# Diagonal and short block lengths of the second mixer as 32-token products, masked into a compact tile

## Chip, cores and metric

The kernel runs on one core of one Trainium2 chip. The metric is device time of one execution in microseconds. A core has a matrix engine (TensorE, PE in the profile; its weight loads stand apart as PEld), a vector engine (DVE), a scalar engine (ACT), a general engine (POOL) and a queue that issues transfers (SP). They run side by side and wait for each other through semaphores.

## What is computed

One step of a two-layer recurrent decoder for 512 prompt tokens and 32 sample tokens (8 sequences of 4). The change lies in the mixer of the second layer, HGRN2, which has 8 heads with 128 key and 128 value channels. For one head and a chunk of tokens, the reference computes attention with a decay that lies between the two tokens:

```python
    def step(S, inp):
        qc, kc, lc, ic = inp
        bc = jnp.cumsum(lc, axis=2)
        diff = bc[:, :, :, None, :] - bc[:, :, None, :, :]
        dec = jnp.exp(jnp.where(mask, diff, -jnp.inf))
        att = jnp.einsum('bhtsk,bhtk,bhsk->bhts', dec, qc, kc)
        o = (jnp.einsum('bhts,bhsv->bhtv', att, ic)
             + jnp.einsum('bhtk,bhkv->bhtv', qc * jnp.exp(bc), S))
```

Around it stand a projection (`xn @ w_in_c`, 32 column blocks of 128), a gate, an output projection and a feed-forward network; the first layer has two other mixers.

## The kernel before

**Layout.** Channels lie on the 128 partitions, tokens along the free dimension (512 prompt, then 32 sample tokens). A projection block is a chain of 128 x 128 weights against 272 tokens at a time, three products for each block of weights (high part of the weights with high and low part of the input, then low part of the weights): tiles `acc`, `wh`, `wl`. ACT makes `wh` from the loaded weights `wf` (line 202), DVE makes `wl` (line 205), SP issues the loads.

**One head (`mix`, from line 1447).** The decayed attention matrix A (tokens s on partitions, tokens t along the free dimension, four blocks of 128 tokens) is built by block length. First the diagonal: products of K and q0, of which the identity keeps the diagonal (tile `d0`, which the profile prints as `d`; trailing numbers are left out). Then for l = 0 to 6 and block length b = 1, 2, 4, ..., 64: products of K with every second block of Q of length b (tile `lv`), of which the mask `lmask[:, l]` keeps those where t lies in the block right after that of s. Between two levels K and Q are multiplied in place by decay products G (K on POOL, line 1477; Q on DVE, line 1478), so a level's products wait for the updates of the level ahead, and those updates wait until that level's products have read K and Q. The masked entries go into A by `copy_predicated` on DVE (line 1480); at b = 64 a plain copy on ACT does it (line 1485). The 32 sample tokens have their own small products (`d0s`; `ps[0:32, 4, 0:16]` at b = 1 and 2).

The products are made on 64 tokens of K by 64 columns: for each of the four blocks of 128 tokens, one product for each half (`g`) writes partitions 0 to 63 or 64 to 127 of the result. Each float32 product is two MATMUL and two LDWEIGHTS in the trace, so 8 products are x16 there.

**What sets the order.** During the heads every product of TensorE is chained in the order in which it is written (`in_order = "all"`). Between the levels a hand-written count of projection products of the next head is placed: `FILL = (27, 13, 13, 24, 10, 23, 5, 9, 4, 19)`, taken by `fill(FILL[l])`. They keep TensorE at work while POOL and DVE update K and Q. On the other engines a scheduler decides the order. `Am` holds two A tiles, used by turns; one quarter of each is cleared once, on POOL (line 1342). Results of the products lie in four PSUM buffers (tag `m`), used in turn. After the levels come transposes of V and K (`tr`, `trs`), the state products `ds` and the outputs `ops<-A,VT`, `ops<-Q,S`, `opsq` and `opsm`; the states of the sample group (`tail`, with `dss`) are done while the next head runs.

Of the kernel before, what the change touches and what calls it, by code (L numbers as in the profile page):

```python
# [11 lines left out]
F32 = mybir.dt.float32  # L12
F32R = mybir.dt.float32r
I32 = mybir.dt.int32
AF = mybir.ActivationFunctionType
OP = mybir.AluOpType
# [65 lines left out]
def consts_np():  # L82
    c = {}
    c["ident"] = np.eye(128, dtype=np.float32)
    b = np.zeros((128, 128), np.float32)
    b[:64, :64] = 1
    b[64:, 64:] = 1
    c["block64"] = b
    c["half32"] = np.repeat(b[:, ::64], 16, axis=1)
    z = np.zeros((128, 4, 128), np.float32)  # L90
    for q in range(4):
        z[32 * q, q, :64] = 1
        z[32 * q + 16, q, 64:] = 1
    c["spread"] = z
    r = np.ones((128, NT), np.float32)
    r[:, 0:SEQ:CH] = 0
    r[:, SEQ::NS] = 0
    c["reset"] = r
    i = np.arange(32)[:, None]
    t = np.arange(32)[None, :]  # L100
    strict, incl = (i < t).astype(np.float32), (i <= t).astype(np.float32)
    same = (i // 4 == t // 4).astype(np.float32)

    def rows(s, n):
        top = np.concatenate([s, n], 1)
        bot = np.concatenate([0 * s, n], 1)
        return np.concatenate([top, bot, top, bot], 0)

    def pair(flip):
        m = np.stack([rows(strict, incl), rows(strict * same, incl * same)], 1)  # L110
        return m.reshape(2, 2, 32, 2, 64)[:, ::-1].reshape(128, 2, 64) if flip else m

    c["smask"] = np.stack([pair(True), pair(False)], 1)
    c["upper"] = np.tile((np.arange(CH) < CH // 2)[:, None], (4, 1)).astype(np.float32)
    sel = np.zeros((32, 8), np.float32)
    sel[np.arange(32), np.arange(32) // 4] = 1
    c["seqsel"] = np.tile(sel, (4, 1))
    c["sum4"] = np.tile(np.eye(32, dtype=np.float32), (4, 1))
    s = np.arange(128)[:, None]
    lv = []  # L120
    for l in range(7):
        b = 1 << l
        t = np.array([x for x in range(128) if (x // b) % 2])[None, :]
        lv.append(((s // b) + 1 == t // b).astype(np.int32))
    c["lmask"] = np.stack(lv, 1)
    return {k: np.ascontiguousarray(v) for k, v in c.items()}


class Build:
# [13 lines left out]
    def fill(self, n):  # L143
        while n and self.work:
            try:
                next(self.work[0])
                n -= 1
            except StopIteration:
                self.work.pop(0)
# [1177 lines left out]
    def mixer1(self, xg):  # L1327
        nc, I = self.nc, self.i
        v = self.v
        TT, STT, TS = nc.vector.tensor_tensor, nc.vector.scalar_tensor_tensor, nc.vector.tensor_scalar  # L1330
        ACT = nc.scalar.activation
        PTT = nc.gpsimd.tensor_tensor
        p = self.open("m1")
        lmask = p.tile([128, 7, 64], I32, name="lmask")
        nc.sync.dma_start(lmask, I["lmask"])
        seqsel = p.tile([128, 8], F32, name="seqsel")
        nc.sync.dma_start(seqsel, I["seqsel"])
        sum4 = p.tile([128, 32], F32, name="sum4")
        nc.sync.dma_start(sum4, I["sum4"])
        Am = [p.tile([128, 4, 128], F32, name=f"A{i}") for i in range(2)]  # L1340
        for i in range(2):
            nc.gpsimd.memset(Am[i][64:128, :, 0:64], 0.0)
        qms = [p.tile([128, NB, 32], F32, name=f"qm{i}") for i in range(2)]
        for i in range(2):
            nc.gpsimd.memset(qms[i], 0.0)
# [18 lines left out]
        def tmp(name, shape=None, bufs=2):  # L1364
            return p.tile(shape or [128, NT], F32, tag=name, name=name, bufs=bufs)

        def blk(z, b, n):
            return z[:, 0:n].rearrange("p (m g b) -> p m g b", g=2, b=b)
# [60 lines left out]
        def tail(h, S0, KVs, G):  # L1429
            Vx = p.tile([96, NB, 128], F32R, tag="Vx", name="Vx")  # L1430
            PTT(Vx, KVs[:, 1, None, :].bitcast(F32).to_broadcast([96, NB, 128]),
                seqsel[0:96, :, None].to_broadcast([96, NB, 128]), OP.mult)
            PTT(S0, S0, G[4][:, SEQ // 4:, None].to_broadcast([128, NB, 128]), OP.mult)
            for q in range(2):
                yield
                bs = slice(4 * q, 4 * q + 4)
                ps = self.ms.tile([128, 4, 128], F32, tag="m", name="dss")
                self.mm(ps, KVs[:, 0], Vx[:, bs])
                TT(S0[:, bs], ps, S0[:, bs], OP.add)
            nc.sync.dma_start(self.o["hS_s"][h], S0)  # L1440
            self.norm_add(oh[h])
            done.append(h)
            if h < len(gates):
                combine(h)

        def mix(h, late):
            K, q0, Q, G, V = heads[h]
            S0 = tmp("S0", [128, NB, 128])
            nc.sync.dma_start(S0, I["hS"][h])
            A = Am[h % 2]  # L1450
            As = tmp("As", [32, 32])
            ps = self.ms.tile([128, 4, 64], F32, tag="m", name="d0")
            for c in range(4):
                for g in range(2):
                    ks = slice(128 * c + 64 * g, 128 * c + 64 * g + 64)
                    self.mm(ps[64 * g:64 * g + 64, c], K[:, ks], q0[:, ks])
            for g in range(2):
                r = slice(64 * g, 64 * g + 64)
                TT(A[r, :, r], ps[r], self.ident[r, None, r].to_broadcast([64, 4, 64]), OP.mult)
            ps = self.ms.tile([32, 32], F32, tag="m", name="d0s")  # L1460
            self.mm(ps, K[:, SEQ:], q0[:, SEQ:])
            TT(As, ps, self.ident[0:32, 0:32], OP.mult)
            for l in range(7):
                b = 1 << l
                ps = self.ms.tile([128, 5, 64], F32, tag="m", name="lv")
                for c in range(4):
                    for g in range(2 if b < 64 else 1):
                        ks = slice(128 * c + 64 * g, 128 * c + 64 * g + 64)
                        self.mm(ps[64 * g:64 * g + 64, c], K[:, ks],
                                blk(Q[:, 128 * c:128 * c + 128], b, 128)[:, :, 1])  # L1470
                if b <= 2:
                    self.mm(ps[0:32, 4, 0:16], K[:, SEQ:], blk(Q[:, SEQ:], b, 32)[:, :, 1])
                n = NT if b <= 2 else SEQ
                m = n // (2 * b)
                g2 = G[b][:, 0:2 * m].rearrange("p (m g) -> p m g", g=2)
                kv, qv = blk(K, b, n), blk(Q, b, n)
                PTT(kv[:, :, 0], kv[:, :, 0], g2[:, :, 1, None].to_broadcast([128, m, b]), OP.mult)  # L1477
                TT(qv[:, :, 1], qv[:, :, 1], g2[:, :, 0, None].to_broadcast([128, m, b]), OP.mult)
                if b < 64:
                    nc.vector.copy_predicated(  # L1480
                        A.rearrange("p c (m g b) -> p c m g b", g=2, b=b)[:, :, :, 1],
                        lmask[:, l, None, :].to_broadcast([128, 4, 64]).rearrange("p c (m b) -> p c m b", b=b),
                        ps[:, 0:4].rearrange("p c (m b) -> p c m b", b=b))
                else:
                    ACT(A[0:64, :, 64:], ps[0:64, 0:4], AF.Copy)
                if b <= 2:
                    nc.vector.copy_predicated(
                        blk(As, b, 32)[:, :, 1], lmask[0:32, l, 0:16].rearrange("p (m b) -> p m b", b=b),
                        ps[0:32, 4, 0:16].rearrange("p (m b) -> p m b", b=b))
                fill(FILL[l])  # L1490
                if late is not None and l in LATE:
                    next(late, None)
# [6 lines left out]
            for z in (V, K):  # L1499
                zt = tmp("KT" if z is K else "VT", [128, 4, 128], 1)  # L1500
                ps = self.ms.tile([128, 4, 128], F32, tag="m", name="tr")
# [7 lines left out]
            ps = self.ms.tile([32, 2, 128], F32, tag="m", name="trs")  # L1509
# [31 lines left out]
            for b in range(NB):  # L1541
                q = 32 * (b % 4)
# [8 lines left out]
            t = tail(h, S0, KVs, G)  # L1551
# [9 lines left out]
        for h in range(8):  # L1561
            if h < 7:
                work.append(project(h + 1))
            for g in GATES[h]:
                work.append(gate(g))
            late = mix(h, late)
            if h < 7:
                drain()
# [26 lines left out]
def prep(x_prompt, x_sample, state_rglru_conv, state_rglru_h, state_rwkv_shift, state_rwkv_S,  # L1595
# [9 lines left out]
    def tiles(w):  # L1605
        w = A(w)
        k, m = w.shape
        return C(w.reshape(k // 128, 128, m // 128, 128).transpose(2, 1, 0, 3)).reshape(m // 128, 128, k)

    d = consts_np()  # L1610
    x = np.concatenate([A(x_prompt).reshape(SEQ, D), A(x_sample).reshape(NB * NS, D)], 0)
    d["xT"] = C(x.T.reshape(KT, 128, NT).transpose(1, 0, 2))
# [75 lines left out]
```

## Time and profile before

| | |
|---|---|
| median of 3 runs | 1539.9 us (1539.0 to 1541.34) |
| profiled execution | 1541.22 us, span 1539.4 us |
| granted TensorE clock, mean | 0.971 |
| ACT busy | 552.5 us (36%) |
| POOL busy | 418.3 us (27%) |
| HBM read, written | 120.65 MB, 11.02 MB |

The span is the time from the first to the last instruction; the profiled execution's own time lies 1.8 us above it. Shares of busy time are means over stages with different limits: the mixer that is changed runs from about 800 to 1080 us of the span. A row "x16" of the timeline is 16 instructions one after the other, from the start of the first to the end of the last. "128*32 128x16" in a row of TensorE is a weight tile of 128 partitions by 32 columns and a moving tile of 16 columns.

### The profile page before, as it was taken

What the parts mean: (1) busy time and instruction counts of PE and PEld (TensorE: products, weight loads), DVE (VectorE), ACT (ScalarE), POOL (GpSimd) and SP (SyncE); (2) the same over time, 40 slices, a digit from 0 to 9 for tenths busy, and PEclk for the clock granted to TensorE, in tenths of its full rate; (3) what the DMA queues carried; (4) which work ended last, traced back from release to release, by engine and by line L of the source; (5) the groups of instructions that cost most, each with busy time, mean ns of one, the idle gap of its engine ahead of it and who ended that gap; (6) DMA issues with size and microseconds to landing.
All of it is one profiled execution on the core that took longest, in us unless ns stands there. A gap on an engine that the chain in (4) does not pass through costs nothing.

```text
span 1539.4 us, 33537 instructions
## 1 busy us (share of the span) xinstructions
PE 1465.2 (95%) x13872; PEld 1408.7 (92%) x13872; DVE 860.2 (56%) x1618; ACT 552.5 (36%) x997; POOL 418.3 (27%) x540
## 2 busy tenths in 40 slices
PE   6967888779999999999999999999999999999998
PEld 6857777669999999999999999999999999999997
DVE  7777555785544344334576667666674433444444
ACT  5634234354433233223352333333453322332224
POOL 3664535542110011001133434444431100110010
PEclk9978989889999999999999999999999999999999
DMA  4224311122232322322231232322242222223221
GB/s 158 70 71 104 105 38 36 49 80 93 83 96 83 90 89 84 96 83 91 85 120 58 85 98 85 106 87 90 97 124 90 89 86 87 90 90 90 84 75 59
DMA packets 92010, 133.86 MB, mean 87 GB/s; under 512 B 28976, under 2 KB 34864, under 8 KB 91728
## 3 DMA queue, kind: packets, MB, share of 16 engines
q1 hardware_dynamic: 91856, 131.71, 27.2%
q8 instruction: 109, 1.79, 0.5%
q14 instruction: 45, 0.37, 0.1%
HBM read 120.65 MB, written 11.02 MB: 86 GB/s over the span
## 4 chain that ended last, share of the span: by engine, by line
PE 84%; DVE 7%; ACT 3%; issue 2%; DMA 2%; POOL 1%; SPq 1%; DVEq 0%; POOLq 0%; ACTq 0%
PE acc L171 74%; PE lv L171 2%; PE ops L171 1%; PE ch L171 1%; DVE Z L842 1%; DVE t L571 0%; PE ds L171 0%; PE tr L1503 0%; DVE W L528 0%; PE nps L171 0%; DVE wl L205 0%; DMA S<-rS 0%; DMA x<-xT 0%; DMA wd<-down 0%; DVE Pd L653 0%
## 5 line engine op out<-in xcount | busy, mean ns | idle before, releaser
L171 PE MATMUL acc<-xg,wh 128*128 128x272 f32 x4544 | 888.1, 293 | 11.7 <-ACT xg L262 7.2
L171 PEld LDWEIGHTS acc<-xg,wh 128*128 128x128 f32 x4544 | 721.7, 191 | 21.7 <-ACT xg L262 7.5
L171 PE MATMUL acc<-xg,wl 128*128 128x272 f32 x2272 | 653.1, 293 | 0.2 <-DVE wl L205 0.2
L202 ACT ACTIVATE wh<-wf 128x512 fp32r<-128x512 f32 (+1 forms) x404 | 250.8, 621 | 655.8 <-PE acc L171 544.3
L171 PEld LDWEIGHTS acc<-xg,wl 128*128 128x128 f32 x2272 | 429.1, 190 | 4.9 <-issue 1.3
L205 DVE TENSOR_TENSOR wl<-wf,wh 128x512 fp32r<-128x512 f32 (+1 forms) x373 | 267.1, 716 | 192.2 <-ACT wh L202 166.2
L1207 POOL TENSOR_TENSOR S<-S,rstd 128x272 f32<-128x272 f32 x88 | 74.3, 845 | 645.3 <-ACT S L1206 645.2
L171 PE MATMUL acc<-h,wh 128*128 128x272 f32 x1280 | 236.9, 288 | 0.0
L171 PEld LDWEIGHTS acc<-h,wh 128*128 128x128 f32 x1280 | 198.0, 188 | 0.0
L171 PE MATMUL acc<-h,wl 128*128 128x272 f32 x640 | 176.7, 287 | 0.0
L171 PEld LDWEIGHTS acc<-h,wl 128*128 128x128 f32 x640 | 118.1, 188 | 0.0
L1210 DVE TENSOR_TENSOR hh<-acc,S 128x272 f32<-128x272 f32 x88 | 38.9, 442 | 127.2 <-PE acc L171 125.3
L171 PE MATMUL acc<-cat,wh 128*128 128x272 f32 (+2 forms) x512 | 100.2, 295 | 2.7 <-ACT wh L202 2.7
L171 PEld LDWEIGHTS acc<-cat,wh 128*128 128x128 f32 x512 | 82.7, 194 | 3.5 <-ACT wh L202 3.1
L1206 ACT ACTIVATE S<-t 128x272 f32<-128x272 f32 x88 | 37.8, 431 | 123.4 <-DVE t L1205 123.4
L1227 DVE TENSOR_TENSOR x<-acc,x 128x272 f32<-128x272 f32 x80 | 35.0, 439 | 83.3 <-PE acc L171 83.0
L1205 DVE TENSOR_TENSOR t<-acc,rstd 128x272 f32<-128x272 f32 x88 | 38.7, 441 | 70.7 <-PE acc L171 70.6
L171 PE MATMUL acc<-cat,wl 128*128 128x272 f32 (+2 forms) x256 | 74.2, 296 | 2.0 <-POOL wl L205 1.0
L280 POOL TENSOR_TENSOR ssq<-ssq,sq 128x544 f32<-128x544 f32 x33 | 46.5, 1410 | 93.4 <-ACT sq L279 93.0
L1477 POOL TENSOR_TENSOR K<-K,G 128x256 f32<-128x256 f32 (+1 forms) x48 | 39.8, 828 | 78.3 <-PE lv L171 78.3
L205 POOL TENSOR_TENSOR wl<-wf,wh 128x512 fp32r<-128x512 f32 x31 | 41.3, 1334 | 40.7 <-ACT wh L202 40.4
L171 PEld LDWEIGHTS acc<-cat,wl 128*128 128x128 f32 x256 | 49.2, 194 | 2.8 <-POOL wl L205 1.4
(341 smaller groups left out, 1506.9 us busy)
## 6 DMA issues: line engine op xcount, KB each, us to landing
wf<-gate SPq DMA_DIRECT2D x88, 256.0 KB
wf<-up SPq DMA_DIRECT2D x88, 256.0 KB
wf<-down SPq DMA_DIRECT2D x72, 256.0 KB
wf<-w_in_c SPq DMA_DIRECT2D x64, 256.0 KB
wf<-w_in_ab SPq DMA_DIRECT2D x44, 256.0 KB
x<-xT SPq DMA_DIRECT2D x16, 272.0 KB
wf<-w_out_ab SPq DMA_DIRECT2D x16, 256.0 KB
S<-hS SPq DMA_DIRECT2D x8, 512.0 KB
```

The source lines that it names most:

```text
L171: return self.seq(self.nc.tensor.matmul(out, lhsT, rhs, start=start, stop=stop, skip_group_check=True), chain)
L202: nc.scalar.activation(wh[:, :n], wf[:, :n], AF.Copy)
L205: eng.tensor_tensor(wl[:, :n], wf[:, :n], wh[:, :n].bitcast(F32), OP.subtract)
L280: eng.tensor_tensor(self.ssq, self.ssq, t, OP.add)
L842: nc.vector.tensor_copy(zc[par][q, e::2], cu[q])
L1205: nc.vector.tensor_tensor(t[:, c], ps, rs()[:, c], OP.mult)
L1206: nc.scalar.activation(S[:, c], t[:, c], AF.Silu)
L1207: nc.gpsimd.tensor_tensor(S[:, c], S[:, c], rs()[:, c], OP.mult)
L1210: nc.vector.tensor_tensor(hh[:, c], ps, S[:, c], OP.mult)
L1227: nc.vector.tensor_tensor(x[:, c], ps, x[:, c], OP.add)
L1477: PTT(kv[:, :, 0], kv[:, :, 0], g2[:, :, 1, None].to_broadcast([128, m, b]), OP.mult)
```

## The change

The products of the diagonal and of b = 1 to 16 are made on 32 tokens of K instead of 64. Each of the four groups of 32 tokens in a block of 128 writes its own 32 partitions of the result, that is, a quarter of the columns of the TensorE array: 32 columns for the diagonal, 16 for a level. At b = 32 there are two products of 32 by 32 for each block of 128, on the first and the third quarter. b = 64 stays.

The results of the diagonal and of b = 1 to 16 are masked into a compact tile `Ad` (128 x 4 x 32) instead of A. After b = 16, four copies on POOL lay the four quarters of `Ad` on the diagonal of A. At b = 32 two copies on ACT write A, in place of a masked copy on DVE. Both A tiles are cleared whole at the start. The mask shrinks to 5 levels of 16.

```diff
-    c["lmask"] = np.stack(lv, 1)
+    c["lmask"] = np.ascontiguousarray(np.tile(np.stack(lv, 1)[0:32, 0:5, 0:16], (4, 1, 1)))
...
-        lmask = p.tile([128, 7, 64], I32, name="lmask")
+        lmask = p.tile([128, 5, 16], I32, name="lmask")
...
-            nc.gpsimd.memset(Am[i][64:128, :, 0:64], 0.0)
+            nc.gpsimd.memset(Am[i], 0.0)
...
-            ps = self.ms.tile([128, 4, 64], F32, tag="m", name="d0")
+            quads = [slice(32 * q, 32 * q + 32) for q in range(4)]
+            ps = self.ms.tile([128, 4, 32], F32, tag="m", name="d0")
             for c in range(4):
-                for g in range(2):
-                    ks = slice(128 * c + 64 * g, 128 * c + 64 * g + 64)
-                    self.mm(ps[64 * g:64 * g + 64, c], K[:, ks], q0[:, ks])
-            for g in range(2):
-                r = slice(64 * g, 64 * g + 64)
-                TT(A[r, :, r], ps[r], self.ident[r, None, r].to_broadcast([64, 4, 64]), OP.mult)
+                for r in quads:
+                    ks = slice(128 * c + r.start, 128 * c + r.stop)
+                    self.mm(ps[r, c], K[:, ks], q0[:, ks])
+            Ad = tmp("Ad", [128, 4, 32])
+            TT(Ad, ps, sum4[:, None, :].to_broadcast([128, 4, 32]), OP.mult)
...
-                    for g in range(2 if b < 64 else 1):
-                        ks = slice(128 * c + 64 * g, 128 * c + 64 * g + 64)
-                        self.mm(ps[64 * g:64 * g + 64, c], K[:, ks],
-                                blk(Q[:, 128 * c:128 * c + 128], b, 128)[:, :, 1])
+                    Kc, Qc = K[:, 128 * c:128 * c + 128], Q[:, 128 * c:128 * c + 128]
+                    if b < 32:
+                        for r in quads:
+                            self.mm(ps[r, c, 0:16], Kc[:, r], blk(Qc[:, r], b, 32)[:, :, 1])
+                    elif b == 32:
+                        for r, t in ((quads[0], quads[1]), (quads[2], quads[3])):
+                            self.mm(ps[r, c, 0:32], Kc[:, r], Qc[:, t])
+                    else:
+                        self.mm(ps[0:64, c], Kc[:, 0:64], Qc[:, 64:128])
...
-                if b < 64:
+                if b < 32:
                     nc.vector.copy_predicated(
-                        A.rearrange("p c (m g b) -> p c m g b", g=2, b=b)[:, :, :, 1],
-                        lmask[:, l, None, :].to_broadcast([128, 4, 64]).rearrange("p c (m b) -> p c m b", b=b),
-                        ps[:, 0:4].rearrange("p c (m b) -> p c m b", b=b))
+                        Ad.rearrange("p c (m g b) -> p c m g b", g=2, b=b)[:, :, :, 1],
+                        lmask[:, l, None, :].to_broadcast([128, 4, 16]).rearrange("p c (m b) -> p c m b", b=b),
+                        ps[:, 0:4, 0:16].rearrange("p c (m b) -> p c m b", b=b))
+                elif b == 32:
+                    for r, t in ((quads[0], quads[1]), (quads[2], quads[3])):
+                        ACT(A[r, :, t], ps[r, 0:4, 0:32], AF.Copy)
                 else:
                     ACT(A[0:64, :, 64:], ps[0:64, 0:4], AF.Copy)
+                if b == 16:
+                    for r in quads:
+                        nc.gpsimd.tensor_copy(A[r, :, r], Ad[r])
```

What this does to the order of instructions is shown at three places of a head. On TensorE, where a head starts (`opsm` ends the head ahead, `d` is the diagonal, `lv` the level b = 1, and the `acc` rows are the next head's projection); lines with - are of before, with + of the change:

```order
 L171 MATMUL opsm<-sum_9503,Oi 128x32
-L171 MATMUL d_10146<-q_9990,K 64x64 x8
-L171 MATMUL d0s<-q_9990,K 32x32
-L171 MATMUL lv<-Q,K 64x64 x8
-L171 MATMUL lv<-Q,K 32x16
+L171 MATMUL d_10199<-q_10043,K 32x32 x16
+L171 MATMUL d0s<-q_10043,K 32x32
+L171 MATMUL lv<-Q,K 32x16 x17
 L171 MATMUL acc<-xg,wh 128x272 x2
 L171 MATMUL acc<-xg,wl 128x272
```

Twice as many products, of half the rows, stand at the same place, and the small product of the sample tokens now has the same shape as the others; nothing else moves on this engine.

On POOL, from the update of K at b = 8 to that at b = 64 in the first head (`G` are decay products of the next head), first before:

```order
L1403 TENSOR_TENSOR G<-G 128x32
L1403 TENSOR_TENSOR G<-G 128x16
L1477 TENSOR_TENSOR K<-K,G 128x16x16
L1403 TENSOR_TENSOR G<-G 128x8
L1403 TENSOR_TENSOR G<-G 128x4
L1477 TENSOR_TENSOR K<-K,G 128x8x32
L1477 TENSOR_TENSOR K<-K,G 128x4x64
```

and now:

```order
L1403 TENSOR_TENSOR G<-G 128x32
L1482 TENSOR_TENSOR K<-K,G 128x16x16
L1403 TENSOR_TENSOR G<-G 128x16
L1496 COPY A_9505<-Ad 32x4x32 x4
L1403 TENSOR_TENSOR G<-G 128x8
L1482 TENSOR_TENSOR K<-K,G 128x8x32
L1403 TENSOR_TENSOR G<-G 128x4
L1482 TENSOR_TENSOR K<-K,G 128x4x64
```

The four copies into A stand between the updates of K at b = 16 and b = 32; two of the G products have moved behind updates of K.

On ACT, in the same stretch of a head (`F`, `K` and `q` belong to the next head, `wh` are the projection's weights, `VT` comes after the levels), first before:

```order
L1384 ACTIVATE K<-fr 128x544
L202 ACTIVATE wh<-wf 128x512 x2
L1390 ACTIVATE q_9990<-fr 128x544
L1485 ACTIVATE A_9505<-lv 64x4x64
L1504 ACTIVATE VT<-tr 128x512
```

and now:

```order
L1384 ACTIVATE K<-fr 128x544
L202 ACTIVATE wh<-wf 128x512
L1491 ACTIVATE A_9505<-lv 32x4x32 x2
L202 ACTIVATE wh<-wf 128x512
L1390 ACTIVATE q_10043<-fr 128x544
L1493 ACTIVATE A_9505<-lv 64x4x64
L1515 ACTIVATE VT<-tr 128x512
```

The two copies of b = 32 stand between the two weight conversions.

## The prediction

> **What bounds the kernel now.** I read the page first: the busy times and the chain of work that ended last.
>
> ```profile
> PE 1465.2 (95%) x13872; PEld 1408.7 (92%) x13872; DVE 860.2 (56%) x1618; ACT 552.5 (36%) x997; POOL 418.3 (27%) x540
> PE 84%; DVE 7%; ACT 3%; issue 2%; DMA 2%; POOL 1%; SPq 1%; DVEq 0%; POOLq 0%; ACTq 0%
> ```
>
> TensorE carries 84% of the chain. This is a mean over the program, so I look at the changed mixer alone: two of eight windows of 35 us between 800 and 1080 us, then who waited for whom in that stretch.
>
> ```profile
> 835.00:870.00 35.00, 35.00 (x395) 32.06 (x395) 23.23 (x49) 12.03 (x25) 15.72 (x19) 1.00 0.28 89
> 870.00:905.00 35.00, 35.00 (x342) 32.94 (x341) 21.12 (x43) 11.33 (x23) 13.57 (x19) 1.00 0.26 83
> ...
> ACT wh L202 <- PE acc L171: 112.7, 49, 6.5
> POOL K L1477 <- PE lv L171: 89.3, 52, 4.2
> DVE wl L205 <- ACT wh L202: 25.0, 28, 1.6
> ```
>
> The columns of a window are PE, PEld, DVE, ACT and POOL busy, clock, DMA share and GB/s. TensorE is never idle, at full clock; DVE has 12 us of 35 free, POOL about 20. The two largest waits are others waiting for TensorE: ACT for a buffer of weights, POOL for the level's products. No wait of TensorE for another engine is among them. So here time is what TensorE's own instructions take, and the chain of one head shows them; its pieces run from one start to the next:
>
> ```profile
> 867.74 0.61 PE d L171 x16
> 868.35 0.18 PE d0s L171 x2
> 868.53 0.78 PE lv L171 x18
> ...
> 842.85 0.79 PE lv L171 x18
> 843.63 1.82 PE acc L171 x13
> 845.46 0.62 PE lv L171 x16
> 847.90 0.62 PE lv L171 x16
> 851.71 0.61 PE lv L171 x16
> 852.32 1.46 PE acc L171 x10
> 853.78 0.62 PE lv L171 x16
> 854.39 3.06 PE acc L171 x23
> 857.46 0.61 PE lv L171 x8
> ```
>
> (The first three belong to the head that follows.) What the change rewrites of a head, diagonal to b = 32, is 0.61 + 0.18 + 0.78 + 0.79 + 0.62 + 0.62 + 0.61 + 0.62 = 4.83 us of TensorE, eight times over 38.6 us. b = 64 (the last row, 0.61) stays.
>
> **How such a batch is priced.** A "pair" is a weight load with its MATMUL. Batches on parts of the array, from timeline rows (start, time, form, count) and the row that follows each:
>
> ```profile
> 865.23 0.64 PE L171 MATMUL opsq<-S,qm 128*32 128x128 f32 x16
> 865.80 0.39 PE L171 MATMUL acc<-xg,wh 128*128 128x272 f32 x1
> ...
> 279.40 0.43 PE L171 MATMUL ops<-Z,W 128*32 128x64 f32 x16
> 279.77 0.52 PE L171 MATMUL acc<-xg,wh 128*128 128x272 f32 x2
> ...
> 217.08 0.73 PE L171 MATMUL jps<-Yt,NTt 32*32 32x16 f32 x64
> 217.74 0.52 PE L171 MATMUL acc<-xg,wh 128*128 128x272 f32 x2
> ...
> 80.44 1.26 PE L171 MATMUL ndps<-KB,W 64*32 64x32 f32 x124
> 81.54 0.25 PE L171 MATMUL ndss<-W,KB 64*32 64x32 f32 x4
> ...
> 229.39 1.05 PE L171 MATMUL jps<-join,Zt 32*32 32x16 f32 x64
> 230.37 0.59 PE L171 MATMUL acc<-xg,wh 128*128 128x272 f32 x1
> ```
>
> First, rounds count, not pairs, as long as pairs lie on different parts: at b = 64 eight pairs on one half take 0.61, at b = 32 sixteen pairs on two halves 0.62. Second, 128x32 weights on the four quarters (the new form) run four abreast: 16 pairs, four rounds, took 0.57 with 128 columns (`opsq`) and 0.37 with 64 (`ops`). The 0.20 between them is 4 rounds of 64 columns, so 64 columns cost 0.05 a round and 0.37 - 4 x 0.05 = 0.17 is fixed: going over, first weights, draining. Third, a floor by pairs: `ndps` made 124 in 1.10 us, 8.9 ns each.
>
> **The change, part by part.** *A level at b = 4, 8, 16*: 32 pairs of 16 columns in 8 rounds. By columns alone 8 x 0.0125 + 0.17 = 0.27. By the floor 32 x 0.0089 = 0.28, plus some 0.11 for going over (estimated from `jps`: 0.66 - 64 x 0.0086) = 0.39. No row shows this form with so few columns. The dear end is the slower `jps`: (0.98 - 0.11) / 64 = 13.6 ns a pair, 0.55 for 32. I take 0.38, nearest to the fast `jps` and `ndps` rows, which have pairs as small as these. *b = 2*, 34 pairs: 0.40. *Diagonal, sample diagonal and b = 1*: 32 + 2 + 34 pairs, now of one weight shape, so the array goes over once. The old rows show what that costs: `d0s`, two pairs, took 0.18. I reckon 2 x 0.38 - 0.11 + 4 x 0.009 = 0.69, for 1.57 before. *b = 32*: 16 pairs on two quarters, 8 rounds of 32 columns: 8 x 0.025 + 0.17 = 0.37.
>
> New sum of a head: 0.69 + 0.40 + 3 x 0.38 + 0.37 = 2.60; saved 4.83 - 2.60 = 2.23 us, over eight heads **17.8 us**. With the cheap end (0.27 a level, 0.29 at b = 2, 0.55 for the first batch) a head is 2.02 and 22.5 us are saved; with 13.6 ns a pair it is 1.03 + 0.57 + 3 x 0.55 + 0.37 = 3.62, and 9.7 us are saved.
>
> *Does the saving reach the end?* The `acc` pieces between levels stay, and the updates of K and Q start when a level ends; cover and cover's need move together. What is new beside TensorE:
>
> ```profile
> 852.41 0.87 POOL L1477 TENSOR_TENSOR K<-K,G 128x256 f32<-128x256 f32 x1 [0.35 <-PE lv L171]
> 853.25 0.47 POOL L1403 TENSOR_TENSOR G<-G 128x8 f32<-128x8 f32 x2
> 854.49 0.67 POOL L1477 TENSOR_TENSOR K<-K,G 128x256 f32<-128x256 f32 x1 [0.76 <-PE lv L171]
> 858.21 0.97 POOL L1477 TENSOR_TENSOR K<-K,G 128x256 f32<-128x256 f32 x1 [3.06 <-PE lv L171]
> ...
> L1495 POOL COPY qm<-Q 128x32 f32<-128x32 f32 x8 | 1.7, 208 | 0.7 <-DVE Q L1478 0.7
> L1477 POOL TENSOR_TENSOR K<-K,G 128x256 f32<-128x256 f32 x40 | 31.6, 790 | 56.5 <-PE lv L171 56.5
> ...
> 853.32 0.63 ACT L202 ACTIVATE wh<-wf 128x512 fp32r<-128x512 f32 x1 [4.27 <-PE acc L171]
> 855.96 0.63 ACT L202 ACTIVATE wh<-wf 128x512 fp32r<-128x512 f32 x1 [2.01 <-PE acc L171]
> 858.10 0.38 ACT L1485 ACTIVATE A<-lv 64x256 f32<-64x256 f32 x1 [0.96 <-PE lv L171]
> ...
> 787.07 0.56 POOL L1342 MEMSET A<- 64x256 f32 x2
> 790.53 1.36 POOL L280 TENSOR_TENSOR ssq<-ssq,sq 128x544 f32<-128x544 f32 x1 [2.27 <-ACT sq L279]
> ```
>
> *Four POOL copies* of 128 elements a partition, each from 0.21 us (a copy of 32 elements) to 0.79 (a product of 256 elements, two sources); I take 0.3, by the copy, since they are copies of half the elements of the other: 1.2 us a head. They also wait for the masked copy of b = 16 on DVE. Behind them in the queue is K's update for b = 32, which TensorE awaits at b = 64 (857.46). From 853.5 (K's update ended at 853.28, one G behind it) to there are 3.9 us; K's update 0.67, a G 0.25 and the 0.25 by which b = 32 gets shorter leave 2.7 for the copies. 1.2 is hidden; without that cover it would be 9.6 us in all. *Two ACT copies* of b = 32 fall into the 2.01 us in which ACT waits for TensorE between two `wh`; at some 0.3 each (b = 64's copy of twice the elements takes 0.38) they cost nothing, and the second `wh`, queued behind them, still waits for TensorE. *Masked copies and diagonal on DVE* shrink to a quarter of the elements, and one copy in six goes. DVE holds TensorE nowhere here, so I count nothing. *Clearing A whole* on POOL lies before 2.27 us of waiting: nothing. *The smaller mask load* is done long before use: nothing.
>
> In the terms of the profiled execution: 1541.2 - 17.8 = 1523.4 us. That execution lies 1.3 above the median of the runs, so the forecast for a median is **1522**.
>
> **Rivals.** *A, pairs at the slower pace.* 13.6 ns a pair as in the second `jps`: 9.7 saved, 1530. The `ops` batch speaks against it: sixteen pairs with four times the columns took 0.37 with all that is fixed. 8%.
>
> *B, TensorE is paced by the instruction.* If the time between two starts didn't depend on columns, doubling the pairs would lose. Its price: `opsq` (0.57 - 0.11) / 16 = 29 ns and a level today (0.62 - 0.11) / 16 = 32 ns, alike although the one has twice the columns. At 32 ns a head takes 214 x 0.032 + 6 x 0.11 = 7.5 us, 2.7 more than now: **1561, slower**. It decides from (4.83 - 0.66) / 214 = 19.5 ns a pair upward. Against it: b = 64, where half the pairs take the same time, and `ndps` at 8.9 ns over 124 pairs. 5%.
>
> The page "TensorE: Matmul & The Clock Gate" of the Trainium skill (Part 1, "Wait — 56ns, not 53.3ns?") states such a rule: start to start never falls under about 25 ns, however few the columns. By that figure the estimate would be 214 x 0.025 + 0.66 = 6.0 us a head, about 1549. The trace disagrees, with 8.9 ns a pair in `ndps`, so I follow the trace.
>
> *C, the copies on POOL become the wait.* At 0.79 each four take 3.2 us for 2.7 of cover: some 0.5 a head late, 4 back, 1526. The wait on DVE would come on top. 5%.
>
> *D, the gain turns into waits for weights.* The projection would run faster than ACT and DVE convert, and the time stays 1540. Against it: ACT waits 112.7 of 280 us for TensorE. 3%.
>
> **How the numbers follow.** Forecast 79%, with its own range of 1517 (columns alone) to 1527; A 8%, B 5%, C 5%, D 3%. The range 1517 to 1531 takes in both ends of the unknown pair and the rivals A and C. A measurement of this kernel tells about 0.2% (3 us) from no change: faster in forecast, A and C, 92%; same in D, 3%; slower in B, 5%.
>
> **What would show it.** In the chain of a head: the `lv` pieces of x32 at 0.35 to 0.40 instead of 0.62, the diagonal to b = 1 together at 0.65 to 0.75 instead of 1.57, the `acc` pieces between them unchanged; TensorE's windows still full and the mixer about 18 us shorter. Pieces of 0.5 or more say A or B. A new wait of `lv` for K, at b = 64 alone, says C; new waits of `acc` for `wh` or `wl` say D. I am wrong outright if the new pieces are as I say and the time hasn't fallen.

## The result, and the profile after

| | median, us | ratio to before, 95% interval |
|---|---|---|
| before | 1539.9 (1539.0 to 1541.68, 5 runs) | |
| changed | 1522.21 (1520.57 to 1524.25, 5 runs) | 0.9881 [0.987, 0.9892] |

17.7 us between the medians; 17.8 had been reckoned, and 1522 forecast. The profiled execution of the changed kernel took 1522.68 us, span 1520.9.

The page of the changed kernel, busy times and chain by engine:

```profile
PE 1446.3 (95%) x14640; PEld 1393.2 (92%) x14640; DVE 837.5 (55%) x1602; ACT 556.5 (37%) x1013; POOL 431.9 (28%) x572
...
PE 86%; DVE 6%; ACT 2%; POOL 2%; issue 2%; DMA 1%; SPq 0%; DVEq 0%; POOLq 0%; ACTq 0%
```

TensorE is 19 us less busy although it issues 768 pairs more (14640 for 13872). Its share of the chain went from 84% to 86%. DVE lost 23 us and POOL gained 14. Two windows of the mixer, columns as before:

```profile
835.00:870.00 35.00, 35.00 (x533) 32.61 (x532) 21.43 (x50) 10.88 (x23) 17.60 (x26) 1.00 0.27 86
870.00:905.00 35.00, 35.00 (x420) 33.46 (x420) 20.96 (x43) 14.08 (x28) 15.01 (x21) 1.00 0.30 102
```

and the waits over the mixer, here from 800 to 1062 us since it ends earlier (who waits for whom: sum in us, number, longest):

```profile
ACT wh L202 <- PE acc L171: 73.6, 39, 5.3
POOL K L1482 <- PE lv L171: 52.2, 40, 3.4
DVE wl L205 <- ACT wh L202: 24.9, 28, 1.6
...
PE lv L171 <- DVE Q L1483: 0.4, 2, 0.2
```

The stage is still full of TensorE, and the others still wait for it. One wait of TensorE is new and small: twice `lv` waits for Q. The chain of one head, from its diagonal to b = 64 (start, time, piece, number of instructions):

```profile
862.11 0.39 PE d L171 x32
862.50 0.01 PE d0s L171
862.51 0.03 PE lv L171
862.54 0.00 PE d0s L171
862.54 0.33 PE lv L171 x23
862.88 3.56 PE acc L171 x27
866.44 0.23 PE dss L171
866.67 0.42 PE lv L171 x34
867.09 1.82 PE acc L171 x13
868.91 0.38 PE lv L171 x32
869.29 1.82 PE acc L171 x13
871.11 0.37 PE lv L171 x32
871.48 3.21 PE acc L171 x24
874.69 0.38 PE lv L171 x32
875.07 1.45 PE acc L171 x10
876.52 0.38 PE lv L171 x16
876.89 3.09 PE acc L171 x23
879.98 0.61 PE lv L171 x8
```

Diagonal, sample diagonal and b = 1 are one piece now, 862.11 to 862.88, 0.77 us for 1.57 before. The levels of 32 pairs take 0.38 for 0.62. The `acc` pieces between them are what they were (1.82, 1.46, 3.06 to 3.09), so the whole change of a head lies in its own batches: 0.77 + 0.42 + 0.38 + 0.37 + 0.38 + 0.38 = 2.70 us for 4.83. (Behind the diagonal the chain passes through 26 of the 36 instructions only; the time is read from start to start and takes in them all.) What runs beside it on POOL and ACT in a head:

```profile
847.05 0.87 POOL L1482 TENSOR_TENSOR K<-K,G 128x256 f32<-128x256 f32 x1 [0.18 <-PE lv L171]
848.04 1.82 POOL L1496 COPY A<-Ad 32x128 f32<-32x128 f32 x4
...
850.11 0.62 POOL L1482 TENSOR_TENSOR K<-K,G 128x256 f32<-128x256 f32 x1
...
848.80 0.55 ACT L1491 ACTIVATE A<-lv 32x128 f32<-32x128 f32 x2 [0.25 <-PE lv L171]
850.04 0.63 ACT L202 ACTIVATE wh<-wf 128x512 fp32r<-128x512 f32 x1 [0.69 <-ACT A L1491]
...
851.75 0.68 PE L171 MATMUL lv<-Q,K 128*64 128x64 f32 x8
```

K's update at 850.11 is the one that b = 64 waits for. It no longer stands idle until TensorE has read K; it starts when the copies and one G product are done, and ends at 850.73, 1.0 us before b = 64 starts at 851.75.

### The profile page after: what moved, and what is told of

It reads as the page before. It is cut to its first block, busy times and chain, and to the rows that moved or that the text cites. A ratio compares the mean times of both kernels' runs of the same rounds, so it can differ in the third digit from the quotient of the medians.

```text
span 1520.9 us, 35106 instructions
## 1 busy us (share of the span) xinstructions
PE 1446.3 (95%) x14640; PEld 1393.2 (92%) x14640; DVE 837.5 (55%) x1602; ACT 556.5 (37%) x1013; POOL 431.9 (28%) x572
## 4 chain that ended last, share of the span: by engine, by line
PE 86%; DVE 6%; ACT 2%; POOL 2%; issue 2%; DMA 1%; SPq 0%; DVEq 0%; POOLq 0%; ACTq 0%
PE acc L171 77%; PE lv L171 2%; PE ops L171 1%; PE ch L171 1%; DVE Z L842 1%; PE nps L171 1%; DVE t L571 0%; PE ds L171 0%; PE tr L1514 0%; DVE W L528 0%; DMA wf<-w_out_ab 0%; DVE Y L655 0%; PE opsm L171 0%; DMA Zs<-vT 0%; DVE cf L1013 0%
## 5 line engine op out<-in xcount | busy, mean ns | idle before, releaser
L1482 POOL TENSOR_TENSOR K<-K,G 128x256 f32<-128x256 f32 (+1 forms) x48 | 36.2, 754 | 44.4 <-PE lv L171 44.3
```

## The experiments

**Theory R**: the gain is TensorE's own. Pairs of small products on different quarters run side by side, so a batch costs its rounds, a floor by pairs and a going over between weight shapes; all else is hidden. **Rivals**: V, the shorter masks on DVE carry part of it; B, TensorE is paced by the instruction; that switching shapes is free; that the POOL copies cost time, or never can.

| run | median, us | ratio to before, 95% interval |
|---|---|---|
| wide_products | 1540.33 | 1.0003 [0.9992, 1.0013] |
| dve_load_back | 1522.6 | 0.989 [0.9873, 0.9907] |
| sample_on_half | 1527.26 | 0.9914 [0.9901, 0.9928] |
| products_twice | 1534.14 | 0.9957 [0.9941, 0.9972] |
| copies_twice | 1536.39 | 0.9985 [0.9971, 0.9999] |
| no_copies | 1522.3 | 0.9889 [0.9876, 0.9903] |
| spread_both | 1519.58 | 0.9876 [0.9863, 0.9889] |
| after_again | 1522.38 | 0.9887 [0.987, 0.9903] |
| spread_both_again | 1519.26 | 0.9869 [0.9854, 0.9884] |
| clears_added | 1532.55 | 0.9956 [0.9941, 0.9971] |

The first four were run together, then the next three, then the last three. `after_again` is the changed kernel itself; all others are edits of it.

### The products alone taken back

```diff
-                    if b < 32:
-                        for r in quads:
-                            self.mm(ps[r, c, 0:16], Kc[:, r], blk(Qc[:, r], b, 32)[:, :, 1])
...
+                    for g in range(2 if b < 64 else 1):
+                        ks = slice(128 * c + 64 * g, 128 * c + 64 * g + 64)
+                        self.mm(ps[64 * g:64 * g + 64, c], K[:, ks],
+                                blk(Q[:, 128 * c:128 * c + 128], b, 128)[:, :, 1])
```

The diagonal likewise; its mask reads `ps[:, :, 0:32]`.

> The changed kernel with the products of before: diagonal and b = 1 to 32 are made on 64 tokens by 64 columns again, while the compact masks, the copies on POOL and ACT and the small mask stay (the masked entries are then the wrong ones; the amount of work on the other engines is that of the change). Theory R (the gain is TensorE's: fewer rounds and fewer switches of weight shape): the pieces of 0.61 to 0.79 us come back in the chain, and the time is that of before, 1538 to 1542 us. Rival V (the relief of DVE by compact masks carries part of the gain): the time stays below 1535.

Measured: no difference from before. The whole rest of the change, with shorter masks and the copies, is worth nothing that can be measured. The chain has the old pieces:

```profile
837.64 0.61 PE d L171 x16
838.25 0.18 PE d0s L171 x2
838.43 0.79 PE lv L171 x18
...
845.63 0.61 PE lv L171 x16
```

### DVE's load given back

```diff
+                    nc.vector.copy_predicated(
+                        spare, lmask[:, l, None, None, :].to_broadcast([128, 4, 4, 16]),
+                        ps[:, 0:4, None, 0:16].to_broadcast([128, 4, 4, 16]))
```

> The changed kernel, with a second masked copy of 256 elements a partition behind each of the 40 compact ones, so that DVE has at least its old load in the heads (40 x 0.43 to 0.75 us = 17 to 30 us more). Theory R: 1520 to 1524 us, as the changed kernel. Rival V: 1528 us or more.

Measured: the time of the changed kernel. The added copies in the mixer (busy us, mean ns):

```profile
L1491 DVE COPY_PREDICATED spare<-lmask,lv 128x256 f32<-128x256 int32 x40 | 17.7, 443 | 0.0
```

The added masked copies cost DVE 17.7 us, the low end of what was expected, and brought its busy time to 854.7 us, 5.5 short of the 860.2 before. Rival V falls on both sides: the relief alone gains nothing, and its loss costs nothing.

### The sample's products on 64 columns

```diff
-            self.mm(ps, K[:, SEQ:], q0[:, SEQ:])
-            TT(As, ps, self.ident[0:32, 0:32], OP.mult)
+            self.mm(ps, K[:, SEQ - 32:], q0[:, SEQ:])
+            TT(As, ps[32:64], sum4[32:64], OP.mult)
...
-                    self.mm(ps[0:32, 4, 0:16], K[:, SEQ:], blk(Q[:, SEQ:], b, 32)[:, :, 1])
+                    self.mm(ps[0:64, 4, 0:16], K[:, SEQ - 32:], blk(Q[:, SEQ:], b, 32)[:, :, 1])
```

The masked copy of the sample tokens reads partitions 32 to 63 accordingly.

> The changed kernel, with only the small products of the sample tokens (sample diagonal, b = 1 and 2) made on 64 columns of weights, so that TensorE changes the weight shape between the batches again. Theory R: each change costs a drain of 0.11 to 0.13 us; the first batch of a head takes 1.13 instead of 0.77 us and b = 2 0.53 instead of 0.42, 0.47 us a head, together 3.8 us: 1526. Rival (rounds alone count, a change of shape is free): 1522 to 1523.

Measured: 1527.26, some 5 us slower than the changed kernel by the ratios (0.9914 to 0.9881, the intervals don't touch). The chain shows where:

```profile
833.13 0.39 PE d L171 x32
833.52 0.23 PE d0s L171 x2
833.75 0.59 PE lv L171 x34
...
838.14 0.59 PE lv L171 x34
```

The first batch takes 0.39 + 0.23 + 0.59 = 1.21 instead of 0.77 and b = 2 0.59 instead of 0.42, with as many pairs. That is 0.61 us a head by the chain, 4.9 in all; 3.8 had been expected. The run has four changes of shape a head more than the changed kernel (three in the first batch, one at b = 2), 0.15 us each, and as many as the kernel before. So a good part of the gain, about a quarter, is not rounds but that all these products now share one weight shape.

### The short products made twice

```diff
-                        for r in quads:
+                        for r in quads + quads:
```

> The changed kernel with every product of b = 1 to 16 made twice into the same place: 32 more pairs in each of 40 batches. Theory R: 32 x 8.5 ns = 0.27 us a batch, 10.9 us in all: 1533. Rival B (paced by the instruction at 25 to 32 ns a pair): 32 to 41 us more, 1554 to 1563. If there were slack on TensorE in the heads: 1522.

Measured: 1534.14, as R says. At b = 2, a row of the timeline and the one behind it, in this run and in the changed kernel (first pair of rows, then second):

```profile
841.58 0.75 PE L171 MATMUL lv<-Q,K 128*32 128x16 f32 x66
842.26 0.52 PE L171 MATMUL acc<-xg,wh 128*128 128x272 f32 x2
```

```profile
906.84 0.49 PE L171 MATMUL lv<-Q,K 128*32 128x16 f32 x34
907.26 0.52 PE L171 MATMUL acc<-xg,wh 128*128 128x272 f32 x2
```

0.68 us from start to start for 66 pairs against 0.42 for 34: 8.1 ns for each of the 32 added. Rival B needed 19.5 or more. The 32 pairs are also eight rounds more, 33 ns each, so this run doesn't tell a floor by the pair from one by the round. The single records of the changed kernel show what a round is worth: two products on the same quarter start 32 ns apart at b = 16 (four pairs a round, 16 columns) and also at b = 32 (two pairs a round, 32 columns); before, with 64 columns, they started 58 ns apart on the same half. So going from 32 to 16 columns shortened nothing: in the chain above the diagonal, with 32 columns, takes 0.39 and a level of as many pairs, with 16, takes 0.38.

### Copies on POOL: none, and twice as many

```diff
-                    for r in quads:
-                        nc.gpsimd.tensor_copy(A[r, :, r], Ad[r])
+                    for r in quads + quads:
+                        cp = nc.gpsimd.tensor_copy(A[r, :, r], Ad[r])
```

with the update of K at b = 32 held behind the last copy; and, in the other run, the copies left out.

> The changed kernel without the four copies on POOL (the diagonal of A stays empty). Theory R: hidden, so 1521 to 1523, as the changed kernel. Rival (the 14 us that POOL spends on them cost time, by delay of K's update or by disturbing DVE): 1519 or less.

> The changed kernel with the four copies on POOL made twice, all eight ahead of the update of K that b = 64 waits for. In the changed kernel that update ends about 1.0 us before b = 64 starts, and the four copies take 1.75 us. Theory R with the cover as it is read there: four more copies come 0.75 us too late, eight heads, 6 us: 1528, and a wait of lv for K at b = 64. Rival (the copies don't reach TensorE at all): 1522.

Without them the time stays, 1522.3: four are free. Eight cost 14 us, more than twice what was expected, and about four fifths of what the change had gained. POOL's timeline in a head of that run:

```profile
849.66 1.82 POOL L1498 COPY A<-Ad 32x128 f32<-32x128 f32 x4
851.56 0.20 POOL L1403 TENSOR_TENSOR G<-G 128x8 f32<-128x8 f32 x1
851.71 2.20 POOL L1498 COPY A<-Ad 32x128 f32<-32x128 f32 x4
853.99 1.00 POOL L1482 TENSOR_TENSOR K<-K,G 128x256 f32<-128x256 f32 x1
```

and TensorE's wait over the mixer, from its waits:

```profile
PEld lv L171 <- POOL K L1482: 14.1, 8, 1.8
```

The place was right (b = 64 waits for K, once a head), the price wrong: the second four took 2.28 us to K's update instead of 1.75, and the update 1.00 instead of 0.62. Those 2.66 us against 1.0 of cover are 1.7 a head.

### Clears in the place of the added copies

In the changed kernel a copy alone takes 0.28 us; those that run beside DVE's `wl` and then its update of Q (two SBUF inputs each) for their whole length take 0.66 to 0.74. That suggested that reading copies stand still while such a product runs.

```diff
+                    for r in quads:
+                        cp = self.order(cp, nc.gpsimd.memset(spare[r], 0.0))
```

> The changed kernel with four clears on POOL (32 partitions by 256 elements, about 0.31 us each, writing only) behind the four copies and ahead of K's update for b = 64, where the doubled copies stood. Theory R with collisions (a POOL copy that meets a DVE product of two SBUF tiles stands still for that time; a clear reads nothing and doesn't): 1.2 us more a head for 1.0 of cover, plus up to 0.4 if K's update meets DVE: 1523 to 1527. Rival (four more POOL instructions in the queue cost what the copies cost): 1534 to 1538.

Measured: 1532.55, between the two and nearer to the rival: the theory with collisions, as it was priced, fails here. POOL, then DVE, in the same head:

```profile
852.89 1.33 POOL L1501 MEMSET spare<- 32x256 f32 x4
854.30 0.79 POOL L1404 TENSOR_TENSOR G<-G 128x8 f32<-128x8 f32 x1
855.05 0.61 POOL L1483 TENSOR_TENSOR K<-K,G 128x256 f32<-128x256 f32 x1
...
853.70 0.69 DVE L205 TENSOR_TENSOR wl<-wf,wh 128x512 fp32r<-128x512 f32 x1 [0.15 <-ACT wh L202]
854.31 0.72 DVE L1392 TENSOR_TENSOR q<-q,fr 128x544 f32<-128x544 f32 x1
855.06 1.18 DVE L1394 TENSOR_TENSOR Q<-q,F 128x544 f32<-128x544 f32 x1
```

The clears took 1.33 us with their gaps and none was lengthened, though `wl` ran beside the last two. But the next instruction that reads, a G product of 8 elements, met `q` and took 0.79 instead of 0.20; in seven of the eight heads it took 0.73 to 0.79. K's update behind it kept its 0.61, and there DVE's product that began with it was the one held up: 1.18, where the mean of the changed kernel is 0.74. So the collision wasn't avoided, only moved: 1.33 + 0.59 = 1.92 against 1.0 of cover, 0.9 a head. The rest of the measured 10 us isn't settled (the waits of `lv` for K make 8.8 us; two executions of the same code differed by 1.4 us ahead of the mixer in the traces).

The Trainium skill, "SBUF — State Buffer", section "Who interferes with whom", says that a Vector instruction with two SBUF inputs contends with a GpSimd instruction that reads SBUF, and not with one that only writes it. The traces agree: 0.28 against up to 0.74 for a copy, 0.30 to 0.31 for every one of the 32 clears.

### A version that uses the array further

```diff
-                        for r, t in ((quads[0], quads[1]), (quads[2], quads[3])):
-                            self.mm(ps[r, c, 0:32], Kc[:, r], Qc[:, t])
+                        for i in (0, 2):
+                            self.mm(ps[quads[i + c % 2], c, 0:32], Kc[:, quads[i]], Qc[:, quads[i + 1]])
                     else:
-                        self.mm(ps[0:64, c], Kc[:, 0:64], Qc[:, 64:128])
+                        z = 64 * (c % 2)
+                        self.mm(ps[z:z + 64, c], Kc[:, 0:64], Qc[:, 64:128])
...
-                        ACT(A[r, :, t], ps[r, 0:4, 0:32], AF.Copy)
+                        for z in range(2):
+                            ACT(A[quads[i], z::2, quads[i + 1]], ps[quads[i + z], z:4:2, 0:32], AF.Copy)
...
-                    ACT(A[0:64, :, 64:], ps[0:64, 0:4], AF.Copy)
+                    for z in range(2):
+                        ACT(A[0:64, z::2, 64:], ps[64 * z:64 * z + 64, z:4:2], AF.Copy)
```

> The changed kernel with the same number of products, but b = 64 spread over both halves of the array (odd blocks of 128 tokens on the upper one) and b = 32 over all four quarters; ACT's copies move the results to their partitions, 4 and 2 instead of 2 and 1. Theory R (rounds count): b = 64 has 4 rounds of 64 columns instead of 8 and falls from 0.61 to 0.38, b = 32 4 rounds instead of 8, from 0.38 to 0.25; 0.35 us a head, 2.8 us: 1519.5. Rival (pairs count, which stay): 1522.

> The version with b = 64 on both halves and b = 32 on all four quarters once more, beside the changed kernel: 2.8 us below it if rounds count, as its trace says (0.34 us a head); the same time if that gain doesn't reach the end.

> The changed kernel once more, beside the next one on the same chip: 1520 to 1524 us by every theory.

Its chain has the two pieces as expected, with the same number of pairs:

```profile
847.09 0.26 PE lv L171 x16
850.41 0.38 PE lv L171 x8
```

0.38 became 0.26 and 0.61 became 0.38, 0.35 us a head. On the same chip its four runs lay between 1519.03 and 1519.5, those of the changed kernel between 1521.13 and 1523.28: 3.1 us between the medians, for 2.8 expected. The intervals of the two ratios still overlap, so it is the trace and the runs side by side that carry this, not the ratios. It is faster than both kernels, and it shows rounds apart from pairs most cleanly.

## Why the prediction was right

- **TensorE bounds the mixer.** Right: taking back its products alone gave all the time back, and DVE's load could come and go.
- **The price of a batch.** 0.38 a level was reckoned, 0.37 to 0.38 measured; b = 32 0.37 and 0.38. b = 2 was 0.42 for 0.40, and the first batch 0.77 for 0.69: this term was mis-sized by 0.08. In the chain `d` alone takes 0.39, and the 36 pairs behind it take 0.38; that the two batches in a row would save the full 0.11 of going over was too much. A head saves 4.83 - 2.70 = 2.13 instead of 2.23 us, eight heads 17.0. In the two traces the mixer, from the first diagonal to the last `opsm`, takes 260.75 and 243.95 us, 16.8 less, and five of the eight heads gain 2.13 or 2.14.
- **What the price was built on.** The 0.0086 us a pair behind its 0.11 for going over stands in no row: it is what is left of the 0.66 when 0.11 is taken off, so the two rest on each other. The changed kernel's trace has 0.11 us from the last start at b = 16 to the start behind it, and the changes of shape in `sample_on_half` cost 0.15 each. The floor was taken to be one of pairs; whether it is that or one of rounds (32 ns, above) stays open. Both give the same time for a level, since its four quarters are used in turn.
- **The size of the whole.** 17.7 between medians and 17.8 reckoned agree better than the steps do. The first batch and b = 2 were 0.8 us too hopeful over eight heads. Two of the heads in which gates are computed gain only 1.9, since `lv` now waits some 0.2 us for Q there, which no term had. The profiled executions differ by 18.5, of which 1.4 arose before the mixer in code that wasn't changed, so the last digits of this agreement are luck.
- **The copies on POOL are hidden.** Right, as their absence shows. Their price was 0.44 on average, not 0.3: the lone price is 0.28, and those that meet DVE take up to 0.78. The cover was nearly right: 2.7 was reckoned, 1.8 is used and 1.0 left. Rival C was nearer than its 5% said: what it needs is not dear copies but twice as many.
- **ACT, clears, mask load: nothing.** No wait of TensorE for ACT is among the waits of this stretch. The second `wh` waits for the copies of b = 32 now (0.69 us, where it had waited for TensorE), and isn't late.
- **Rivals A and B**, pairs at 13.6 or 32 ns: the new batches run at 8 to 9 ns a pair when 0.11 is taken off for going over, and doubled products cost 8.1. The floor of about 25 ns that the Trainium skill gives (the page named in the prediction) doesn't hold for this form here: the pairs of one round start some 7 ns apart. Between two pairs on the same quarter the trace has 32 ns.
- **Rival D**, waits for weights: none appeared. ACT's waits for TensorE ahead of `wh` fell from 112.7 to 73.6 us and are still the largest; 15.9 us of its waits are now put down to DVE's update of Q and 5.5 to the copies of b = 32.

## What to carry to other kernels

Small products that have a part of the array to themselves cost their rounds, not their number: halving the rows and doubling the pairs was worth some 1.5 of the 2.1 us that each head gained, because the number of rounds stayed and each became shorter, from 58 to 32 ns. Below 32 columns there was no more to gain here, and only fewer rounds helped, as in the last version. Giving neighbouring small products one weight shape is worth as much attention; here it was the other 0.6 us, about a quarter of the gain. Work moved to an engine beside the path is free as long as its cover lasts, but its lone price is not the one to compare with the cover: read what the other engines do in the stretch into which it slides.

## What the runs showed of the hardware that was not expected

- A round of products on quarters of the array took 32 ns with 32 columns and also with 16.
- A POOL copy that lasts 0.28 us alone took up to 0.78 beside DVE products of two SBUF inputs. Behind clears, which weren't held up, the next reading instruction was (0.79 instead of 0.20), so the delay passed on to what read next. It can also fall on DVE: its product took 1.18 instead of 0.74 beside an update of K that kept its 0.61.
- ACT copies from partitions 64 to 127 of PSUM to partitions 0 to 63 of A cost nothing extra that shows. Their durations (min, median, max in ns) in the second run of the version above, spread_both_again, half of them such copies:

```profile
L1496 ACT ACTIVATE A<-lv x16: 270/272/274, 823.3 to 1036.6; 64x128 f32<-64x128 f32 x16
```

and those in place, in the changed kernel:

```profile
L1491 ACT ACTIVATE A<-lv x16: 267/268/270, 821.0 to 1036.6; 32x128 f32<-32x128 f32 x16
```
